# Beginning the first feed-forward with the context's w1 and w3 products, and seven products for every latent pair

## The chip, the cores and the metric

The kernel runs on one core of a Trainium2 chip. Its metric is the device time of one execution in microseconds. Engines are named as in the profile: PE (matrix products), DVE (vector), ACT (activation), POOL (GpSimd), SP (issues most DMAs). One program is one in-order stream for each engine; the streams wait on each other with semaphores.

## The reference, cut to what matters

One layer of a diffusion trunk with 1024 latent tokens and 256 context tokens of width 1024. The change lies in the first of its two feed-forwards, with F = 2816 hidden columns (22 blocks `f` of 128):

```python
def rms_norm(x, w):
    y = x * lax.rsqrt(jnp.mean(x * x, axis=-1, keepdims=True) + EPS)
    return y * w
def modulate(h, shift, scale):
    return h * (1.0 + scale[:, None, :]) + shift[:, None, :]
def swiglu(h, w1, w3, w2):
    return (jax.nn.silu(h @ w1) * (h @ w3)) @ w2

m_l = split(silu(c) @ ada_w + ada_b, 9)          # latents: 9 groups of 1024 modulation columns
m_c = split(silu(c_ctx) @ ada_w + ada_b, 9)      # context
x = x + 0.5 * m_l[2] * swiglu(modulate(rms_norm(x, norm1_w), m_l[0], m_l[1]), ffn1_w1, ffn1_w3, ffn1_w2)
ctx = ctx + 0.5 * m_c[2] * swiglu(modulate(rms_norm(ctx, norm1_w), m_c[0], m_c[1]), ffn1_w1, ffn1_w3, ffn1_w2)
...  # token mixing (retention and gated linear attention), second feed-forward, final norm
```

## The kernel before

All tensors lie transposed in SBUF: features on the 128 partitions, tokens along the free axis. The latents are two groups of 512 tokens (`tg` 0 and 1), the context one of 256 (`tg` 2).

**Products.** A float32 product is made of three products of fp32r parts. `split` makes a high part on ACT (`whi`, `hh`; a copy to fp32r) and a low part, the rest, on DVE or POOL (`wlo`, `hl`; a TENSOR_TENSOR subtraction of the high part from its source). So a block of weights of 128x512 costs one load, one ACT copy and one subtraction before PE can use all of it. `mm3` and `proj` issue hi·hi, hi·lo and lo·hi.

**Classic blocks and pairs.** A block f done the classic way takes w1 and w3, each over 8 slices of the features and 2 token groups: 2 x 8 x 2 x 3 = 96 matmuls of 128x512. A pair of blocks (f, f+1) can instead be done by `chain`, with the seven products of a 2x2 block scheme over sums of weight halves (`seven_w`) and sums of token-group halves (the four T tiles, made once by `t_make`): 7 x 4 x 3 = 84 matmuls for w1 and 84 for w3. One chain's result goes through ACT (silu) or DVE (multiply) into stores to DRAM.

**Opening.** `first1`, with an order for PE, DVE and ACT written by hand, takes f = 0 to 3 the classic way. It begins with the norm of the first latent group and with modulation columns (8, 0, 9, 1, ...) made on PE (`pe_load`, `pe_sums`, `pe_turn`: eight matmuls of a 32-wide condition with a 512 KB block of `ada_w`, then a turn of the row into a column); as soon as the norm's slice 0 is there, blocks 0 to 3 begin for token group 0, slice by slice. Then, in `phase_ffn1`'s loop, the same four blocks follow for token group 1, while `t_make` makes the T tiles on DVE and ACT. Other modulation columns are made on DVE by a custom multiply-and-add reduction over a 128x1024 tile (line 523 in the profile).

**Pairs and the rest.** `hidden(4)` runs the chains of pairs f = 4, 6, ..., 20; then PE does the w2 sums of the latents (`back6`), whose start the prediction uses as a mark. After that `ctx_ffn` does the whole context feed-forward: 44 units of w1 or w3 (24 matmuls of 128x256 each; the weights loaded a second time) with the w2 sums of a pair of blocks between them. In that stretch two low halves of every unit's four are given to POOL (`hl<-s,hh`, line 422). It is followed by products of the second norm.

**Order.** `Recorder` records a stretch of the program, plans an order for all engines from costs of its own (with `LEAD`, a DMA rate of 300 GB/s, a landing time `DLAT`, and DVE and POOL treated as sharing a port), and emits it. Outside recorded stretches a scheduler with priorities orders the instructions.

Of the kernel before, what the change touches and what calls it, by code (L numbers as in the profile page):

```python
# [41 lines left out]
class Root:  # L42
    def __init__(self, shape, dtype, make=None, real=None, pool=None, slot=None, ready=-1e9):
        self.shape, self.dtype, self.make, self.real, self.pool, self.slot = shape, dtype, make, real, pool, slot
        self.log, self.todo, self.end, self.ready = [], 0, ready, ready


class View:
# [25 lines left out]
    def __getitem__(self, key):  # L74
        k = key if isinstance(key, tuple) else (key,)
        dims, off = [], list(self.off)
        for i, (s, n, a) in enumerate(self.dims):
            j = k[i] if i < len(k) else slice(None)
            if isinstance(j, slice):
                b, e, _ = j.indices(s)  # L80
                off[a] += b * n
                dims.append((e - b, n, a))
            else:
                off[a] += j * n
# [81 lines left out]
class Recorder:  # L166
    def __init__(self, trunk):
        t = self.trunk = trunk
        self.nc, self.tc, self.ops, self.group, self.slots, self.kept = t.nc, t.tc, [], None, {}, {}
# [39 lines left out]
    def add(self, eng, call, outs, ins, name, a, k):  # L209
# [4 lines left out]
        if eng == "PE":  # L214
# [5 lines left out]
            else:  # L220
                cost = size / 600 + 0.01 if size > 64 else size * 0.0011
        elif eng == "SP":
# [10 lines left out]
        op.kind = kind  # L233
        op.port = eng == "POOL" or name in SHARED and not any(self.psum(v.root) for v in ins)
# [12 lines left out]
    def link(self):  # L247
        event, touched = None, defaultdict(list)
        for i, op in enumerate(self.ops):
            op.i = i  # L250
            for v, w in [(v, False) for v in op.ins] + [(v, True) for v in op.outs]:
                r, (a, b, c, d) = v.root, v.box
                keep = []
                for e in r.log:
                    (p, q, s, t), o, ow = e
                    hit = p < b and a < q and s < d and c < t
                    hit = hit or self.psum(r) and not (w and ow)
                    if hit and (w or ow) and o is not op:
                        op.pre.add(o)
                    if not (w and a <= p and q <= b and c <= s and t <= d and o is not op):  # L260
                        keep.append(e)
                r.log = keep + [((a, b, c, d), op, w)]
                if r not in op.roots:
# [5 lines left out]
                    if isinstance(r.pool, Pool):  # L269
                        op.pre.add(r.pool.event)  # L270
# [32 lines left out]
    def run(self):  # L303
# [3 lines left out]
        free = {"PE": 0.0, "DVE": LEAD, "ACT": LEAD, "POOL": LEAD, "SP": LEAD}  # L307
        port = {"DVE": LEAD, "POOL": LEAD}
        kind = True
        cand, table, pipe, order = [o for o in self.ops if not o.left], None, LEAD, []  # L310
        while cand:
            best = None
            byeng = defaultdict(list)
            for o in cand:
# [28 lines left out]
            else:  # L343
# [9 lines left out]
                if o.eng == "SP":  # L353
                    pipe = max(pipe, s) + o.bytes / 300e3
                    o.end = max(pipe, s) + DLAT
# [37 lines left out]
class Trunk:  # L393
    def __init__(self, ctx, tc, I, out, outt):
# [9 lines left out]
        self.sds = [self.nc.dram_tensor(f"sd{i}", (2, NP, P, 512), F32, kind="Internal").ap() for i in range(2)]  # L404
        for n, s in (("cgk", (256, CTX)), ("crk", (512, CTX)), ("cgv", (CTX, 512)), ("crv", (CTX, 512)), ("p89d", (P, CTX)), ("s0g", (4, P, P)),
# [24 lines left out]
    def consts(self):  # L430
# [3 lines left out]
        self.ident = self.tile(cp, [P, P], F32, "ident")  # L434
        self.ones = self.tile(cp, [P, P], F32, "ones")
# [6 lines left out]
    def cond_load(self):  # L442
        self.cs = [self.cond_row("c")]
        self.junk = self.tile(self.dp, [P, D], mybir.dt.bfloat16, "junk")

# [5 lines left out]

    def cond_silu(self):
        for o in (0, 512):
            t = self.cs[-1][:, o:o + 512]
            self.nc.scalar.activation(t, t, AF.Silu)

    def pe_cond(self, pool):
# [10 lines left out]
        self.ab1 = self.tile(pool, [P, 2], F32, "ab1")  # L468
        nc.vector.scalar_tensor_tensor(out=self.ab1, in0=self.col("ada_b")[:, 8:10], scalar=1.0, in1=self.col("norm1_w")[:, 0:2],
# [15 lines left out]
    def pe_copy(self, ps, n, pool):  # L485
        s = self.tile(pool, [P, n], F32, f"csum{n}", 256 // n)
        self.nc.scalar.copy(s, ps[:, :n])
        return [s[:, o:o + P] for o in range(0, n, P)]

# [3 lines left out]

    def pe_out(self, j, src, dve=False):
        if dve and j >= 8:
            k, m, ts = j - 8, self.mods, self.nc.vector.tensor_scalar
# [1902 lines left out]
```

## Time and profile before

| | |
|---|---|
| runs | 2087.51, 2082.72, 2086.14 us; median 2086.14 |
| span of the profiled execution | 2087.0 us (no other time is listed for it) |
| first product of the first feed-forward | 15.12 us |
| first chain (f = 4) | 114.37 us |
| `back6` | 460.33 us |
| context stage (`ctx_ffn`) | 642.33 us |
| PE busy, DVE busy over the span | 2071.6 us, 1471.9 us |

The timeline lists each instruction, or a run of equal ones, with its start and its duration; the starts of successive matmuls are closer than their durations, since matmuls are pipelined. The table by windows gives each engine's busy time in a stretch, the granted PE clock (PEclk, 1.00 is full) and the DMA share and rate. A group's row gives duration in ns of one instruction and a count.

### The profile page before, as it was taken

The numbers are of one execution on the slowest core, as the hardware profiler recorded it, in microseconds if no ns is written. First come the engines' busy times: TensorE is split into PE (matmuls) and PEld (weight loads), VectorE is DVE, ScalarE is ACT, GpSimd is POOL, SyncE is SP. The second block draws the span as 40 slices with busy tenths as digits, with TensorE's granted clock in tenths as the row PEclk, the third lists the DMA queues.
The fourth block names the chain that finished last, engine by engine and source line by source line (L and its number), as shares of the span: only waits on it lengthen the run. The fifth ranks groups of instructions, "written<-read, shape, count | busy, mean of one in ns | idle before, by whom it ended". The sixth has DMA issues, their size and how long they took to land.

```text
span 2087.0 us, 34162 instructions
## 1 busy us (share of the span) xinstructions
PE 2071.6 (99%) x12352; PEld 1763.0 (84%) x12352; DVE 1471.9 (71%) x2660; ACT 973.3 (47%) x1818; POOL 199.3 (10%) x195
## 2 busy tenths in 40 slices
PE   9999999999999999999999999999999999999998
PEld 6888888888889999998788988888888888888888
DVE  6889999666776445765577478767776666765586
ACT  5433433435544445566475246444434344344553
POOL 0000000000015665001021001000000000010000
PEclk9999999999999999999999999999999999999999
DMA  9277667449886553674233233242344444477774
GB/s 348 84 241 237 232 217 256 149 165 371 277 289 222 181 183 115 195 219 129 76 108 98 79 91 105 90 162 81 112 156 147 144 163 157 151 235 229 218 237 151
DMA packets 201082, 370.58 MB, mean 178 GB/s; under 512 B 23249, under 2 KB 35921, under 8 KB 200785
## 3 DMA queue, kind: packets, MB, share of 16 engines
q1 hardware_dynamic: 200768, 368.33, 53.7%
q8 instruction: 97, 1.59, 0.3%
q14 instruction: 73, 0.59, 0.1%
q10 hardware_dynamic: 144, 0.07, 0.0%
HBM read 292.68 MB, written 67.24 MB: 172 GB/s over the span
## 4 chain that ended last, share of the span: by engine, by line
PE 77%; DVE 10%; DMA 8%; issue 3%; ACT 1%; SPq 0%; DVEq 0%; POOLq 0%; ACTq 0%
PE psa L147 18%; PE psa L426 10%; PE psa L428 10%; PE psa L427 10%; PE psb L147 9%; PE psb L427 7%; PE psb L428 7%; PE psb L426 7%; DVE junk L523 2%; DVE wlo L422 2%; DMA raw<-in_w 2%; DMA raw<-sd 2%; DVE hl L422 1%; DMA raw<-gd 1%; DMA hl<-sd 1%
## 5 line engine op out<-in xcount | busy, mean ns | idle before, releaser
L421 ACT ACTIVATE whi<-raw 128x512 fp32r<-128x512 f32 x371 | 233.9, 631 | 502.7 <-issue 160.6
L422 DVE TENSOR_TENSOR wlo<-raw,whi 128x512 fp32r<-128x512 f32 x371 | 254.1, 687 | 178.0 <-ACT whi L421 175.6
L426 PE MATMUL psa<-hh,whi 128*128 128x512 f32 x684 | 267.0, 390 | 1.2 <-ACT s L738 0.6
L428 PE MATMUL psa<-hh,wlo 128*128 128x512 f32 x684 | 266.3, 389 | 0.0
L427 PE MATMUL psa<-hl,whi 128*128 128x512 f32 x684 | 266.2, 389 | 0.0
L427 PE MATMUL psb<-hl,whi 128*128 128x512 f32 x568 | 221.6, 390 | 0.5 <-DVE hl L422 0.3
L428 PE MATMUL psb<-hh,wlo 128*128 128x512 f32 x568 | 221.3, 390 | 0.2 <-DVE wlo L422 0.2
L426 PE MATMUL psb<-hh,whi 128*128 128x512 f32 x568 | 221.1, 389 | 0.0
L426 PEld LDWEIGHTS psa<-hh,whi 128*128 128x128 f32 x684 | 128.4, 188 | 28.9 <-ACT s L711 1.7
L147 DVE TENSOR_TENSOR wlo<-raw,whi 128x512 fp32r<-128x512 f32 (+1 forms) x140 | 88.5, 647 | 90.8 <-ACT whi L147 80.1
L147 PE MATMUL psa<-hl,whi 128*128 128x512 f32 x384 | 152.5, 397 | 0.0
L147 PE MATMUL psa<-hh,whi 128*128 128x512 f32 x384 | 152.3, 397 | 0.0
L147 PE MATMUL psa<-hh,wlo 128*128 128x512 f32 x384 | 152.2, 396 | 0.0
L428 PEld LDWEIGHTS psa<-hh,wlo 128*128 128x128 f32 x684 | 128.4, 188 | 26.6
L427 PEld LDWEIGHTS psa<-hl,whi 128*128 128x128 f32 x684 | 128.5, 188 | 26.3
L422 POOL TENSOR_TENSOR hl<-s,hh 128x512 fp32r<-128x512 f32 x88 | 132.4, 1530 | 145.2 <-DVE hl L422 81.1
L147 ACT ACTIVATE whi<-raw 128x512 fp32r<-128x512 f32 (+1 forms) x140 | 82.5, 599 | 119.7 <-PE psa L147 94.1
L427 PEld LDWEIGHTS psb<-hl,whi 128*128 128x128 f32 x568 | 106.6, 188 | 24.7 <-DVE hl L422 2.7
L428 PEld LDWEIGHTS psb<-hh,wlo 128*128 128x128 f32 x568 | 106.6, 188 | 23.1 <-DVE wlo L422 1.2
L426 PEld LDWEIGHTS psb<-hh,whi 128*128 128x128 f32 x568 | 106.6, 188 | 22.2
L428 PE MATMUL psa<-hh,hl 128*128 128x256 f32 x392 | 111.1, 284 | 0.0
L426 PE MATMUL psa<-hh,hh 128*128 128x256 f32 x392 | 111.1, 283 | 0.0
(443 smaller groups left out, 4820.4 us busy)
## 6 DMA issues: line engine op xcount, KB each, us to landing
raw<-in_w SPq DMA_DIRECT2D x242, 256.0 KB, 3.3
s<-in_w SPq DMA_DIRECT2D x198, 256.0 KB, 3.7
gd<-s SPq DMA_DIRECT2D x154, 256.0 KB, 2.8
ada<-in_adaT SPq DMA_DIRECT2D x60, 512.0 KB, 4.6
raw<-gd SPq DMA_DIRECT2D x91, 256.0 KB, 3.5
sd<-s SPq DMA_DIRECT2D x44, 256.0 KB, 2.7
raw<-sd SPq DMA_DIRECT2D x44, 256.0 KB, 3.2
hh<-in_w SPq DMA_DIRECT2D x44, 256.0 KB, 4.0
```

The costliest lines, as they stand in the source:

```text
L147: self.rec.add(self.eng, lambda: f(*map(get, a), **{x: get(v) for x, v in k.items()}), outs, ins, name, a, k)
L421: nc.scalar.activation(hi, src, AF.Copy)
L422: (eng or nc.vector).tensor_tensor(out=lo, in0=src, in1=hi.bitcast(F32), op=ALU.subtract)
L426: mm(ps, wa[0], xa[0], start=start, stop=False, skip_group_check=more)
L427: mm(ps, wa[0], xa[1], start=False, stop=False, skip_group_check=more)
L428: return mm(ps, wa[1], xa[0], start=False, stop=stop, skip_group_check=more)
L523: nc.vector.tensor_tensor_reduce(out=self.junk, in0=t, in1=self.cs[s], scale=1.0, scalar=self.col("ada_b")[:, j:j + 1], op0=ALU.mult, op1= ...
```

## The change

The kernel now opens with the context. `ctx_open` loads the context (1 MB, in a new layout `ctxP`, four loads) ahead of the first column's tile, makes its norm, and makes all 16 columns of modulation groups 0 and 1 on PE (ten before). It then does 14 units (f = 0 to 6) slice by slice into seven PSUM banks, in the order of the table `OPEN`: a pair (i, q) loads half q of unit i, a positive number loads two column tiles, a negative one makes the two columns and the norm of a slice. `ctx_rest` does the remaining 30 units one after the other; of each unit's two 128x512 weight halves one low part is made on DVE and one on POOL. The gated products go to DRAM (`cgd`, 22 stores). Beside it `lat_open`, a generator that is advanced once for each f, issues the latents' loads, squares, norms and `t_make`; in its norms `norm_a` and `norm_b` are one SCALAR_TENSOR_TENSOR each on DVE. All of this is one recorded stretch, planned with a lead of 0, a DMA rate of 345 GB/s, a landing of 2 us, and without the shared port of DVE and POOL (`apart=False`). The first weight halves of `hidden`'s first chain (`seven_w`) are part of it.

Then `hidden(0)` does all eleven pairs by chains. The later `ctx_ffn` does only the w2 sums: it loads w2 and `cgd`. There POOL makes one of four low parts of a pair's w2. Modulation groups 0 and 1 are dropped from the columns made on DVE (72 reductions in place of 84).

```diff
 class Recorder:
-    def __init__(self, trunk):
+    def __init__(self, trunk, lead=None, rate=300e3, land=None, apart=True):
...
-        op.port = eng == "POOL" or name in SHARED and not any(self.psum(v.root) for v in ins)
+        op.port = self.apart and (eng == "POOL" or name in SHARED and not any(self.psum(v.root) for v in ins))
...
+                    if o.eng == "SP" and not self.apart:
+                        t = max(t, pipe - BACKLOG)
...
+    def ctx_open(self, xp, n1):
...
+        for k in range(KD):
+            for i in range(NW):
+                w, h = self.wslice(ws[i], k), self.h[2][k]
+                for j, (u, v) in enumerate(((0, 0), (1, 0), (0, 1))):
+                    nc.tensor.matmul(acc[i], w[u], h[v], start=k + j == 0 and i % 2 == 0, stop=k == KD - 1 and j == 2,
+                                     skip_group_check=True)
+        return acc
+
+    def ctx_g(self, f, p1, p3):
+        t = self.stile()[:, :CTX]
+        self.nc.scalar.activation(t, p1, AF.Silu)
+        self.nc.vector.tensor_tensor(out=t, in0=p3, in1=t, op=ALU.mult)
+        self.nc.sync.dma_start(self.cgd[f], t)
+
+    def ctx_rest(self, xp, n1, lat):
+        acc = self.ctx_open(xp, n1)
+        load = lambda w: [self.load_half(w[:, 512 * q:512 * q + 512], None, self.nc.gpsimd if q else None) for q in range(2)]
+        units = [w[f] for f in range(NW // 2, NF) for w in (self.w1, self.w3)]
+        ws = [load(units.pop(0))]
+        for f in range(NW // 2):
+            self.ctx_g(f, acc[2 * f], acc[2 * f + 1])
+        next(lat)
+        for f in range(NW // 2, NF):
+            ps = []
+            for _ in range(2):
+                if units:
+                    ws.append(load(units.pop(0)))
+                ps.append(self.psA()[:, :CTX])
+                self.proj(ws.pop(0), 2, ps[-1])
+            self.ctx_g(f, *ps)
+            next(lat, None)
+        for _ in lat:
+            pass
...
-            ws = self.first1((xp, xp, None), n1)
-            t_steps = self.t_make(xp, tp)
-            for f in range(4):
-                self.c_silu(f, 1, self.H(ws[2 * f], 1), True)
-                next(t_steps)
-                self.c_mul(f, 1, self.H(ws[2 * f + 1], 1))
-                if f % 2:
-                    next(t_steps)
...
+        rec = Recorder(self, 0.0, 345e3, 2.0, False)
...
+        self.ctx_rest(xp, nn, self.lat_open(xp, nn, swap))
+        ready = self.seven_w(self.w1, 0, True)
+        rec.run()
...
-        self.hidden(4, lambda: mods(MPER), True)
+        self.hidden(0, lambda: mods(MPER), True, ready)
...
-            self.ctx_ffn(units, norms, last)
+            self.ctx_ffn(norms)
...
-PECOL = (8, 0, 9, 1, 2, 3, 4, 5, 6, 7)
+PECOL = tuple(8 * i + k for k in range(8) for i in (1, 0))
-EMODS = ((5, (0,)), (2, (0, 1)), (1, (1,)), (0, (1,)), (4, (0, 1)), (3, (0, 1)), (7, (0,)), (6, (0,)))
+EMODS = ((5, (0,)), (2, (0, 1)), (4, (0, 1)), (3, (0, 1)), (7, (0,)), (6, (0,)))
-WARM = (18, 4)
+WARM = 30
+NW = 14
+BACKLOG = 3
```

In the order of instructions, counted over the whole program, PE loses 48 matmuls of 128x512 and gains 48 of 32x128 (six columns); the number of 128x256 ones by fp32r parts is the same. From the middle of the chains after the context stage on, the order is the same on all engines.

**PE at the start, before.** In these rows line 482 makes the sums of columns 8, 0 and 9, line 491 turns them, line 1198 keeps PE busy, and line 1204 is the first product of the latents.

```order
L482 MATMUL psb_161<-ada_69_197,ccol_185 32x128 x8
L482 MATMUL psa_241<-ada_70_200,ccol_185 32x128 x8
L491 MATMUL psb_159<-cols_80,csum_87_242 128x2
L491 MATMUL psa_162<-cols_80,csum_88_243 128x2
L1198 MATMUL psa_158<-ones_83 128x128 x4
L1204 MATMUL psa_274<-hh_16_114,wh_148 128x512
L1204 MATMUL psa_274<-hh_16_114,wl_149 128x512
L482 MATMUL psb_161<-ada_73_206,ccol_185 32x128 x8
```

**PE at the start, after.** Recorded instructions all carry line 147; `hh_23` is the high part of the context's normed slice 0.

```order
L147 MATMUL psb_175<-ada_17_139,ccol_134 32x128 x8
L147 MATMUL psb_188<-ada_18_148,ccol_134 32x128 x8
L147 MATMUL psb_175<-cols_80,csum_197 128x2
L147 MATMUL psb_188<-cols_80,csum_205 128x2
L147 MATMUL psb_223<-ada_42_161,ccol_134 32x128 x8
L147 MATMUL psa_234<-hh_23_221,whi_202 128x256
L147 MATMUL psa_234<-hh_23_221,wlo_212 128x256
L147 MATMUL psa_234<-hh_23_221,whi_210 128x256
```

The third column's sums stand ahead of the first product now, and the products are of 256 tokens.

**DVE before the first chain, before.** This is the stretch of `t_make` (`t1l`, lines 1119 and 1123) with the first chains' weight parts (`wlo`, line 690) between.

```order
L1119 TENSOR_TENSOR x_131_470<-x_131_470,x_10_93 128x512
L422 TENSOR_TENSOR wlo_1141<-raw_1131,whi_1140 128x512
L690 TENSOR_TENSOR raw_1131<-raw_1137,raw_1131 128x512
L422 TENSOR_TENSOR t1l_184_841<-x_131_470,t1h_183_840 128x512
L1119 TENSOR_TENSOR x_135_515<-x_135_515,x_11_95 128x512
L422 TENSOR_TENSOR wlo_1146<-raw_1137,whi_1145 128x512
L422 TENSOR_TENSOR t1l_186_843<-x_135_515,t1h_185_842 128x512
```

**DVE where the latents' norms begin, after.** `s_1262` is the gate of f = 9 (it needs the sixth of the 30 units from PE); the rows on `x_161` to `x_163` are the first norms, and their group goes on below it for 114 rows in all up to the first chain's w1.

```order
L147 TENSOR_TENSOR wlo_1303<-raw_1164,whi_1290 128x512
L147 TENSOR_TENSOR nacc_1204<-nacc_1204,nsq_1300 128x512
L147 TENSOR_TENSOR nacc_1204<-nacc_1204,nsq_1308 128x512
L147 TENSOR_TENSOR s_1262<-psa_1258,s_1262 128x256
L147 SCALAR_TENSOR_TENSOR x_161_739<-x_161_739,mod_88,nrb_1315 128x512
L147 SCALAR_TENSOR_TENSOR x_162_753<-x_162_753,mod_88,nrb_1315 128x512
L147 SCALAR_TENSOR_TENSOR x_163_767<-x_163_767,mod_88,nrb_1315 128x512
```

The norms and the T tiles now share DVE with the weights' low parts and gates of the context's units.

**POOL, the first large instructions before and after.** Before, the first ones are low parts of the context stage; in after, low parts of the units in `ctx_rest`.

```order
L1665 TENSOR_TENSOR nr_4952<-nr_4952,mhalf_85 128x2
L422 TENSOR_TENSOR hl_1322_5968<-s_5842,hh_1321_5967 128x512
L422 TENSOR_TENSOR hl_1328_5992<-s_5844,hh_1327_5991 128x512
L422 TENSOR_TENSOR hl_1334_6016<-s_5875,hh_1333_6015 128x512
```

```order
L147 TENSOR_TENSOR wlo_843<-raw_727,whi_828 128x512
L147 TENSOR_TENSOR wlo_950<-raw_856,whi_939 128x512
L147 TENSOR_TENSOR wlo_1026<-raw_879,whi_1012 128x512
L147 TENSOR_TENSOR wlo_1086<-raw_899,whi_1070 128x512
```

Of POOL's 88 large subtractions 41 are left: 30 of them stand in the opening, 11 in the context stage.

More of the change, by code (lines that the diff above doesn't have):

```diff
@@ L450, in cond_row @@
         return t
[L452 to L455, printed above, removed]
     def pe_cond(self, pool):
@@ new lines, in ctx_norm, with col_sums @@
+        for t in (acc, sq):
+            for o in (0, CTX):
+                nc.tensor.matmul(pr[:, :CTX], self.ones, t[:, o:o + CTX], start=t is acc and not o, stop=t is sq and o > 0)
+        rb = self.scr(n1, "nacc", 1)[:, :CTX]
+        nc.scalar.activation(rb, pr[:, :CTX], AF.Ln, bias=eps, scale=1.0 / D)
+        nc.scalar.activation(rb, rb, AF.Exp, scale=-0.5)
+        return rb
+    def col_sums(self, pc, o, j, sm, turn, to):
+        self.pe_sums(pc, o, self.cur.pop(j))
+        self.nc.scalar.copy(sm, pc[:, o:o + P])
+        return self.pe_turn(turn, to, sm)
```

549 lines of the change are left out of this document (215 added, 334 removed).

## The prediction, written before the changed kernel was run

> **What bounds the kernel now.** I read the page first: shares of busy time and the slices.
>
> ```profile
> span 2087.0 us, 34162 instructions
> PE 2071.6 (99%) x12352; PEld 1763.0 (84%) x12352; DVE 1471.9 (71%) x2660; ACT 973.3 (47%) x1818; POOL 199.3 (10%) x195
> ...
> DVE  6889999666776445765577478767776666765586
> POOL 0000000000015665001021001000000000010000
> ```
>
> PE is busy for 99% of the span, so on the whole only fewer or cheaper matmuls help. But DVE is at 80 to 90% and more in slices 3 to 7, the opening and the chains of the pairs, and POOL is silent there; it works only in slices 12 to 15, the context stage. Next the table by windows, for four stages (first chain; the other pairs up to `back6`; `back6` with what follows it; context stage) and two samples.
>
> ```profile
> core 0: us, PE busy (x) PEld busy (x) DVE busy (x) ACT busy (x) POOL busy (x), PEclk, DMA share, GB/s
> 114.37:133.42 19.05, 19.05 (x86) 15.78 (x85) 18.64 (x31) 8.31 (x15) 0.00 (x0) 1.00 0.82 271
> 133.42:460.33 326.91, 326.08 (x1430) 267.20 (x1428) 288.51 (x490) 126.28 (x222) 1.64 (x1) 1.00 0.64 212
> 642.33:865.72 223.39, 223.38 (x1741) 217.67 (x1740) 117.30 (x182) 115.63 (x231) 124.73 (x84) 1.00 0.55 179
> 700.00:750.00 50.00, 50.00 (x420) 50.00 (x419) 20.44 (x28) 25.59 (x51) 35.89 (x24) 1.00 0.58 184
> 2.00:30.00 28.00, 25.89 (x197) 17.85 (x196) 16.97 (x34) 17.60 (x33) 0.00 (x0) 1.00 1.02 380
> ```
>
> In the first chain DVE works 18.64 of 19.05 us: PE and DVE bind there together. In the context stage it works only 117.30 of 223.39, with POOL's help. Third, PE's timeline at the stage marks.
>
> ```profile
> start us, us, engine line op out<-in xcount [idle before <-releaser]
> 11.57 0.64 PE L482 MATMUL psb<-ada,ccol 128*32 128x128 f32 x16
> ...
> 15.12 0.50 PE L1204 MATMUL psa<-hh,wh 128*128 128x512 f32 x1 [0.51 <-ACT hh L621]
> ...
> 32.76 0.39 PE L1204 MATMUL psa<-hh,wh 128*128 128x512 f32 x1
> ...
> 37.93 0.39 PE L1204 MATMUL psa<-hh,wh 128*128 128x512 f32 x1
> ...
> 114.37 0.39 PE L426 MATMUL psa<-hh,whi 128*128 128x512 f32 x1
> ...
> 133.41 0.39 PE L426 MATMUL psb<-hh,whi 128*128 128x512 f32 x1
> ...
> 460.33 0.39 PE L426 MATMUL psa<-hh,whi 128*128 128x512 f32 x1
> ```
>
> From these: a chain of 84 matmuls takes 133.41 − 114.37 = 19.04 us, 0.2267 each. The 18 chains up to `back6` take 460.33 − 114.37 = 345.96, or 19.22 each with what they lose. A matmul of 256 tokens takes 50.00 / 420 = 0.119 us (0.1195 when counted over longer stretches). From 32.76 to 37.93 PE does 18 products (4.08) and one column: 1.09 us for a column.
>
> **The balance.** Let T be the start of the first chain after the change. Then 22 chains follow, 422.8 us at 19.22, then the rest, without the context's w1 and w3: 44 units x 24 = 1056 matmuls x 0.1195 = 126.2 us that leave a stage in which PE never waits. So the change in time is T + 422.8 − 460.3 − 126.2 = T − 163.7. All hangs on whether the first chain starts before 163.7 us.
>
> **T by PE alone.** Removed: 8 products x 8 slices x 6 of 512 tokens for f = 0 to 3 (384) against 4 chains (336): 48 x 0.2267 = 10.9 us saved. Added: six columns x 1.09 = 6.5. Start: ahead of the first column stand 1.05 MB of context, where 2.1 MB of latents stood; at the 380 GB/s of the window from 2 to 30 that is 2.8 us earlier, 8.8 for the columns and, with the same 3.55 us from there (15.12 − 11.57), 12.4 for the next work. From there PE has 336 products of 256 tokens (14 units) = 40.2 and 14 columns = 15.3: the opening block ends at 67.9. The 30 other units, 720 x 0.1195 = 86.0, and the small products of two latent norms (some 2 us each, an estimate from the eight of 284 ns and the eight of 239 that one norm takes in the opening, below) end at 157.9. That is T if PE waits for nothing: 157.9 − 163.7 = −5.8, or 2081.2.
>
> ```profile
> L599 PE MATMUL psb<-ndiag,ones 128*128 128x128 f32 x8 | 1.1, 284 | 0.0
> L583 PE MATMUL psb<-ones,nacc 128*128 128x1 f32 x8 | 0.9, 239 | 0.0
> ```
>
> The opening's transfers: 28 weight halves (7.3 MB), 16 column tiles (8.4) and the context (1.0), 16.8 MB, at 380 GB/s 44 us; they land by about 47, and PE is at its last column pair at about 50. That covers it, barely; if PE lost a tenth of the rate, it would wait 4 to 5 us.
>
> **T by DVE.** The order on DVE tells more. Up to the gate of f = 9 (`s_1262`) DVE waits for PE: that row needs six of the 30 units, 67.9 + 17.2, 2.0 for the first norm's products and 0.7 for ACT and the gate itself: 87.8. Only behind it, in DVE's order, stand the latents' norms, the T tiles, ten modulation reductions and the other units' low halves, 114 rows down to the low part of the first chain's w1. Their prices are pitches from DVE's dense timeline and the group of reductions:
>
> ```profile
> 615.87 0.68 DVE L422 TENSOR_TENSOR hl<-hl,hh 128x512 fp32r<-128x512 f32 x1
> 616.47 0.68 DVE L878 TENSOR_TENSOR s<-psa,s 128x512 f32<-128x512 f32 x1
> 617.08 0.74 DVE L884 SCALAR_TENSOR_TENSOR x<-s,mod,x 128x512 f32<-128x512 f32 x1
> 617.74 0.68 DVE L422 TENSOR_TENSOR wlo<-hh,whi 128x512 fp32r<-128x512 f32 x1
> 618.34 0.68 DVE L422 TENSOR_TENSOR hl<-hh,hh 128x512 fp32r<-128x512 f32 x1
> 618.94 4.15 DVE L884 SCALAR_TENSOR_TENSOR x<-s,mod,x 128x512 f32<-128x512 f32 x3
> 623.02 1.77 DVE L422 TENSOR_TENSOR hl<-hl,hh 128x512 fp32r<-128x512 f32 x1
> 624.71 0.74 DVE L884 SCALAR_TENSOR_TENSOR x<-psa,mod,x 128x512 f32<-128x512 f32 x1
> ...
> L523 DVE CUSTOM_DVE_ANT_0 junk<-ada,condc,cols x54: 1266/1276/1286, 24.0 to 362.4; 128x1024 bf16<-128x1024 f32 x54
> ```
>
> 40 SCALAR_TENSOR_TENSOR x 0.66 (617.08 to 617.74) = 26.4; 39 TENSOR_TENSOR x 0.60 = 23.4; 10 gates of 256 elements x 0.34 (their 0.41, below, less the overlap of 0.07 that the larger ones show) = 3.4; 10 reductions x 1.24 (1.276 less some overlap) = 12.4; the last one's end 0.7: 66.3 us. So DVE alone gives 87.8 + 66.3 = 154.1, only 3.8 us less than PE's 157.9. Whatever DVE loses beyond 3.8 us, the first chain starts later, and PE, which runs ahead of its low halves and gates, waits.
>
> **What POOL costs DVE.** 21 of POOL's 30 low halves fall beside these 114 rows. What that costs is seen where POOL's first large instructions begin, at 619.08, in the DVE rows above.
>
> ```profile
> 619.08 6.86 POOL L422 TENSOR_TENSOR hl<-s,hh 128x512 fp32r<-128x512 f32 x4 [81.12 <-DVE hl L422]
> ...
> L422 POOL TENSOR_TENSOR hl<-s,hh x88: 1285/1640/1806, 619.1 to 817.9; 128x512 fp32r<-128x512 f32 x88
> L984 DVE TENSOR_TENSOR s<-psa,s x22: 408/410/425, 651.0 to 829.5; 128x256 f32<-128x256 f32 x22
> ```
>
> From 618.94 to 624.71 DVE does three SCALAR_TENSOR_TENSOR and one TENSOR_TENSOR, 2.58 us by pitch, in 5.77: 3.19 lost to about three POOL instructions, 1.06 each. The 22 gates that read one PSUM operand stay at 408 to 425 ns while POOL runs; those don't pay. Of the 66 us some 50 (the first two terms, two SBUF operands) are like those that pay, so I take 0.75 x 1.06 = 0.80 for each: 21 x 0.80 = 16.8. Ends: 0 (if POOL always falls beside reductions and gates; a gain is excluded, since POOL's 21 halves are not among DVE's rows any more) and 22.3 (1.06 each). So T = 154.1 + 16.8 = 170.9, +7.2 against 163.7, 2094.2 by the profiled span. The median of the runs is 0.9 below that span: 2093.3.
>
> [...]
>
> **Small parts.** SP: each of the 22 stores of a gate waits for DVE, and the weights of later units are queued behind it; the loads behind `s_1262`'s store serve units five or six further on, 15 us of PE work, while landing takes 3 to 4, so I price it at nothing; without that cover each store would cost PE up to 3 us. ACT has some 60 us of copies, squares and norms in 90 us of `ctx_rest`: hidden. The context stage after: per pair PE has 48 x 0.1195 = 5.7 us, DVE 3 low parts and a split (2.4), the loads 1.3 MB (3.4 at 380 GB/s): hidden; uncovered, it would cost under 1 us per pair. The 12 reductions that go (15 us of DVE) lie in the last chains, where DVE has air: nothing, at best 1 us.
>
> **The rivals.** (1) *PE stays the bound*: POOL falls beside gates, reductions and DVE's waits. T = 157.9, 2081.2, as a median 2080. For it: PE's 99%; against it: DVE's 154.1 leaves 3.8 us, so it decides at 0.18 us per POOL instruction, a sixth of what the row shows. (2) *Half the contention*, 0.45 us each: T = 154.1 + 9.5 = 163.6, no change, 2086. For it: POOL's instructions take 1.64 at the median against 1.285 alone, so part of the conflict is paid by POOL. (3) *PE waits and its clock falls*. After two waits of 0.21 and 1.63 us the trace has this:
>
> ```profile
> 1024.60 0.33 PE L147 MATMUL psb<-zq,zk 128*32 128x32 f32 x16 [1.63 <-issue]
> ...
> 1025.00:1027.00 2.00, 2.00 (x23) 1.57 (x19) 1.96 (x5) 0.34 (x2) 0.00 (x0) 0.59 0.03 8
> 1027.00:1029.00 2.00, 2.00 (x49) 1.28 (x49) 0.51 (x3) 0.39 (x3) 0.00 (x0) 0.56 0.00 0
> ```
>
> Granted clock 0.59 and 0.56 for 4 us: 1.7 us of work lost. If PE waits 13 us in `ctx_rest` in pieces of 1 to 3, five such episodes cost 8.5: 2102. The waits will rather be short, one per unit, and PE's work has slack behind DVE then; so less likely. [...] (4) *The opening doesn't feed PE*: transfers at nine tenths of the rate, +5 on rival 1's way, hidden on DVE's only in part: 2086 to 2100, within the others.
>
> **How the numbers follow.** DVE bound with contention, 2087 to 2099 (0.3 to 1.06 us each), 0.46; rival 1 0.26; rival 2 0.18; rival 3 0.10. 0.2%, about what a measurement here tells from no change, is 4.2 us: faster is under 2082, slower over 2090.3. Faster is rival 1: 0.26. Same: rival 2 and 0.04 of the first case, 0.22. Slower: 0.42 + 0.10 = 0.52. The time is that of the likeliest, 2093. The range takes in rival 1 with 3 us of uncertainty on PE's sum (2077.5) and ends at rival 3's 2102.5; some 1 in 10 lies on either side.
>
> **What the profile after would show.** First product at 12.4; the last of the 14 units at 67.9 (if it is later than 72, the transfers bound it). First chain at 171; `back6` 423 us later, at 594. In 90 to 170 us DVE busy over 95% and PE at 85 to 90%, its waits ended by DVE's low halves or POOL's; DVE's `wlo` rows there at about 1 us in place of 0.685, POOL's at 1.6. Wrong would be: PE without waits up to 158 (rival 1); DVE's rows at 0.69 beside POOL; a granted clock under 0.9 between 90 and 170 (rival 3); or a loss behind `back6`, where I expect none.

## The result, and the profile after

The changed kernel takes 2119.3 us (median of four runs, 2119.03 to 2120.25) against 2085.4 for the kernel before: a ratio of 1.0167, interval 1.0152 to 1.0181. It is slower, as forecast, but by 34 us where 7 had been predicted. The page of the changed kernel, its head and three of its rows over the 40 slices:

```profile
span 2117.2 us, 34420 instructions
...
PE 2077.4 (98%) x12438; PEld 1776.4 (84%) x12438; DVE 1516.4 (72%) x2710; ACT 986.3 (47%) x1820; POOL 133.7 (6%) x148
...
DVE  5799999766666577774678467868866676665676
ACT  4644334343344545565665345534433434344553
POOL 0341000000000002011011102000000000010000
```

The span is 30.2 us longer, and PE's busy time only 5.8 us: the rest is PE's waiting. (A run's time lies some 2 us above its span, 2119.03 and 2117.2 here. So the profiled execution before, with a span of 2087.0, was one of about 2089, over 3 us above the median of its kernel; the prediction compared the two without this step and put the median 0.9 below the span. For this reason the account below adds up to 30 us and not to 34.) POOL now works in slices 2 to 4 of the opening. PE's timeline at the marks (start, duration, instruction):

```profile
15.28 0.47 PE L147 MATMUL psa<-hh,whi 128*128 128x256 f32 x1 [0.77 <-ACT hh L147]
...
187.49 0.40 PE L439 MATMUL psa<-hh,whi 128*128 128x512 f32 x1
...
211.32 0.39 PE L439 MATMUL psb<-hh,whi 128*128 128x512 f32 x1
...
611.88 0.39 PE L439 MATMUL psa<-hh,whi 128*128 128x512 f32 x1
```

These are the first product, the first chain, the second chain and `back6`. Together with the ends of the stages they give this account. `prod(4)` is the one product of the latents' w2 sums that is left for after the context stage; 126.2 us of work moved from the context stage to the front:

| stretch | before, us | after, us | change |
|---|---|---|---|
| to `back6` | 460.3 + 126.2 | 611.9 | +25.4 |
| `back6` and what follows it | 182.0 | 179.5 | -2.5 |
| context stage with prod(4) | 223.4 - 126.2 | 108.2 | +11.0 |
| the rest, to PE's last matmul | 1214.4 | 1210.9 | -3.5 |

So two stretches are to be explained. Of the last row 1.7 us is the half clock near 1025 us that the prediction shows in the trace before; the clock of the trace after is full throughout this stretch up to PE's last matmuls. The rest of that row and the second row were not followed up. For the first stretch, the table by windows of the changed kernel:

```profile
core 0: us, PE busy (x) PEld busy (x) DVE busy (x) ACT busy (x) POOL busy (x), PEclk, DMA share, GB/s
10.00:30.00 20.00, 18.73 (x207) 15.38 (x207) 9.87 (x22) 9.51 (x21) 0.00 (x0) 0.83 1.04 396
30.00:68.00 38.00, 38.00 (x406) 36.34 (x405) 27.10 (x51) 22.52 (x44) 3.24 (x2) 1.00 0.83 297
68.00:95.00 27.00, 25.21 (x207) 24.61 (x207) 16.63 (x28) 16.23 (x32) 11.19 (x8) 1.00 0.81 259
95.00:187.50 92.50, 77.34 (x572) 75.95 (x571) 86.07 (x115) 44.91 (x81) 37.60 (x22) 0.89 0.64 209
```

From 95 us to the first chain DVE is busy for 93%, and PE waits 15.2 us and runs at a granted clock of 0.89, which costs another 8.5. PE's list of waits from 12 to 200 us says for whom (us in total, times, longest; two entries of under 1 us are left out):

```profile
PE psa L147 <- DVE wlo L147: 11.2, 4, 5.1
PE psb L147 <- DVE ndiag L147: 5.7, 5, 3.2
PE psa L439 <- ACT s L703: 2.9, 1, 2.9
```

These are DVE's low halves, the small scalings (`ndiag`) of the latents' norms, and an ACT copy (`s`) inside the first chain. And DVE's groups from the gate of f = 9, done at 93.7, to the first chain show why it is late (busy us and mean ns stand after the count):

```profile
L147 DVE TENSOR_TENSOR wlo<-raw,whi 128x512 fp32r<-128x512 f32 x22 | 19.1, 882 | 0.9 <-ACT whi L147 0.9
L510 DVE CUSTOM_DVE_ANT_0 junk<-ada,condc,cols 128x1024 bf16<-128x1024 f32 x10 | 14.6, 1462 | 0.1
L147 DVE SCALAR_TENSOR_TENSOR x<-x,mod,nrb 128x512 f32<-128x512 f32 x16 | 14.5, 938 | 1.5 <-ACT nrb L147 1.5
L147 DVE SCALAR_TENSOR_TENSOR hl<-x,mod,hh 128x512 fp32r<-128x512 f32 x12 | 11.7, 997 | 0.0
L147 DVE TENSOR_TENSOR s<-psa,s 128x256 f32<-128x256 f32 x11 | 4.5, 414 | 3.0 <-PE psa L147 3.0
L147 DVE TENSOR_SCALAR ndiag<-ident,nr 128x128 f32<-128x128 f32 x4 | 3.0, 780 | 0.9 <-POOL nr L147 0.9
```

`wlo` takes 882 ns on average, the norm's instructions 938 and 997, where 684 and 745 are their times alone (shown with the second experiment); the gates, with one operand in PSUM, take 414, where those of the kernel before took 410 at the median. Row by row, 21 instructions are lengthened, 20.3 us together, and POOL does 21 subtractions in this stretch. Each of the 21 began while POOL was in a subtraction, and its extra time is what was left of that subtraction, less 0.13 or 0.19 us. One pair of rows, from the timelines of POOL and DVE:

```profile
103.78 2.46 POOL L147 TENSOR_TENSOR wlo<-raw,whi 128x512 fp32r<-128x512 f32 x1 [2.42 <-ACT whi L147]
105.02 1.76 DVE L147 SCALAR_TENSOR_TENSOR hl<-x,mod,hh 128x512 fp32r<-128x512 f32 x1
```

The subtraction (2.46 us here, where the shortest in the kernel before took 1.29, so POOL loses time too) ends at 106.24, 1.22 us after the DVE row began, and this row takes 1.02 us longer than the 0.74 of its kind.

### The profile page after: what moved, and what is told of

Same layout as the page of the kernel before. It is cut to its first block, busy times and chain, and to the rows that moved or that the text cites. A ratio compares the mean times of both kernels' runs of the same rounds, so it can differ in the third digit from the quotient of the medians.

```text
span 2117.2 us, 34420 instructions
## 1 busy us (share of the span) xinstructions
PE 2077.4 (98%) x12438; PEld 1776.4 (84%) x12438; DVE 1516.4 (72%) x2710; ACT 986.3 (47%) x1820; POOL 133.7 (6%) x148
## 4 chain that ended last, share of the span: by engine, by line
PE 90%; DVE 5%; DMA 3%; ACT 1%; issue 1%; POOL 0%; SPq 0%; POOLq 0%; DVEq 0%; ACTq 0%
PE psa L147 21%; PE psa L439 10%; PE psa L440 10%; PE psa L441 10%; PE psb L147 10%; PE psb L440 9%; PE psb L441 9%; PE psb L439 9%; DMA raw<-in_w 2%; DVE x L147 1%; DVE hl L147 1%; DVE wlo L147 1%; PE psa L1962 0%; DVE wlo L435 0%; DVE nt L147 0%
## 5 line engine op out<-in xcount | busy, mean ns | idle before, releaser
L439 PE MATMUL psa<-hh,whi 128*128 128x512 f32 x692 | 269.4, 390 | 2.1 <-ACT hh L434 1.5
L440 PE MATMUL psa<-hl,whi 128*128 128x512 f32 x692 | 269.4, 389 | 0.4 <-DVE hl L435 0.4
L441 PE MATMUL psa<-hh,wlo 128*128 128x512 f32 x692 | 269.4, 389 | 0.0
L147 PE MATMUL psa<-hh,wlo 128*128 128x512 f32 (+1 forms) x648 | 230.9, 357 | 11.2 <-DVE wlo L147 11.2
L147 PE MATMUL psa<-hh,whi 128*128 128x512 f32 (+1 forms) x648 | 230.7, 357 | 0.8 <-ACT hh L147 0.8
L147 PE MATMUL psa<-hl,whi 128*128 128x512 f32 (+1 forms) x648 | 230.2, 356 | 0.0
L147 ACT ACTIVATE whi<-raw 128x512 fp32r<-128x512 f32 (+1 forms) x209 | 125.1, 608 | 151.6 <-PE psa L147 103.5
L439 PEld LDWEIGHTS psa<-hh,whi 128*128 128x128 f32 x692 | 129.8, 188 | 29.6 <-ACT hh L434 1.7
L440 PEld LDWEIGHTS psa<-hl,whi 128*128 128x128 f32 x692 | 129.9, 188 | 27.6 <-DVE hl L435 0.9
L441 PEld LDWEIGHTS psa<-hh,wlo 128*128 128x128 f32 x692 | 129.9, 188 | 27.0
L147 PEld LDWEIGHTS psa<-hh,wlo 128*128 128x128 f32 x648 | 126.7, 196 | 26.1 <-DVE wlo L147 11.9
L147 PEld LDWEIGHTS psa<-hh,whi 128*128 128x128 f32 x648 | 126.5, 195 | 16.8 <-ACT hh L147 1.0
L147 PEld LDWEIGHTS psa<-hl,whi 128*128 128x128 f32 x648 | 126.5, 195 | 14.1 <-issue 0.2
```

The lines of the kernel that those rows point to most:

```text
L147: self.rec.add(self.eng, lambda: f(*map(get, a), **{x: get(v) for x, v in k.items()}), outs, ins, name, a, k)
L439: mm(ps, wa[0], xa[0], start=start, stop=False, skip_group_check=more)
L440: mm(ps, wa[0], xa[1], start=False, stop=False, skip_group_check=more)
L441: return mm(ps, wa[1], xa[0], start=False, stop=stop, skip_group_check=more)
```

## Experiments on the opening

Theory A: DVE's in-order stream sets the first chain, and POOL's instructions hold it up. Rivals: loads, or PE's own stream.

**All low halves on DVE.**

```diff
-        load = lambda w: [self.load_half(w[...], None, self.nc.gpsimd if q else None) for q in range(2)]
+        load = lambda w: [self.load_half(w[...], None, None) for q in range(2)]
```

> All low halves of the 30 units of ctx_rest are made on DVE, none on POOL. In the trace of the changed kernel 21 DVE instructions between the gate of f = 9 (93.4 us) and the first chain (187.5) lasted 0.66 to 1.14 us longer than their kind, 20.3 us together, each beside one POOL instruction. Theory A (DVE's in-order stream sets the start of the first chain, and POOL's instructions hold it up): DVE gains 20.3 and takes on 21 x 0.60 = 12.6, first chain at about 180, time about 2111 to 2113, and no DVE TENSOR_TENSOR of 512 over 0.75 us there. Rival B (loads, which wait on SP for buffers, or PE's own stream set it): first chain within 2 us of 187.5, time 2118 to 2121. If the long DVE instructions are only waits by another name, DVE just gets 12.6 us more: first chain at 200, 2131.

2103.9 us, ratio 1.0087 (1.0072 to 1.0102), first chain at 173.96: 13.5 us earlier, though DVE does 30 instructions more. The same window of this kernel:

```profile
95.00:187.50 92.50, 83.66 (x614) 79.87 (x613) 89.01 (x153) 51.28 (x94) 1.40 (x1) 0.96 0.68 221
```

No DVE row is lengthened any more (`wlo` takes 684 ns on average, the norm's instructions 743 and 746). The gain is larger than theory A's 7.7 (20.3 less 12.6 for 21 more low halves): the gate of f = 9 also came 1.4 us earlier, and DVE's waits behind it fell from 6.3 to 3.3 us; PE's clock is 0.96 in place of 0.89. The rivals fall.

**POOL's instructions stay, but read nothing.** The low part of one half of each unit's weights is left out; POOL writes zeros in its place.

```diff
+        if eng and self.blank:
+            eng.memset(lo.bitcast(F32), 0.0)
+        else:
             (eng or nc.vector).tensor_tensor(out=lo, in0=src, in1=hi.bitcast(F32), op=ALU.subtract)
```

> Opening and context stage as changed, but the low part that POOL makes of half of every unit's weights is left out: POOL writes zeros there (a memset), in the same places, and reads nothing. So DVE has the same work as in the changed kernel and POOL's instructions stay in number. Theory A with its mechanism (a DVE instruction with two SBUF operands waits while a POOL instruction reads SBUF): no DVE instruction of 512 elements over 0.8 us in 94 to 187 us, first chain at 187.5 - 20.3 = 167, to 172 if PE's waits set it, time 2098 to 2104. Rival (the long DVE instructions come from POOL's writes or its mere presence, or cost nothing): some stay long, first chain after 178, 2110 to 2121.

2105.0 us, ratio 1.0089 (1.0074 to 1.0105), first chain at 171.52. DVE's groups from 87 us to there, the same kinds as above:

```profile
L147 DVE TENSOR_TENSOR wlo<-raw,whi 128x512 fp32r<-128x512 f32 x23 | 15.4, 684 | 0.9 <-ACT whi L147 0.7
L513 DVE CUSTOM_DVE_ANT_0 junk<-ada,condc,cols 128x1024 bf16<-128x1024 f32 x10 | 12.8, 1276 | 0.0
L147 DVE SCALAR_TENSOR_TENSOR x<-x,mod,nrb 128x512 f32<-128x512 f32 x16 | 11.3, 745 | 0.2 <-ACT nrb L147 0.2
L147 DVE SCALAR_TENSOR_TENSOR hl<-x,mod,hh 128x512 fp32r<-128x512 f32 x12 | 8.7, 745 | 0.5 <-ACT hh L147 0.5
L147 DVE TENSOR_TENSOR s<-psa,s 128x256 f32<-128x256 f32 x11 | 4.6, 418 | 0.1
L147 DVE TENSOR_SCALAR ndiag<-ident,nr 128x128 f32<-128x128 f32 x7 | 2.3, 414 | 0.0
```

Every kind with two operands in SBUF is back at its time alone. From the gate of f = 9 to the first chain it is 74.2 us in place of 94.1, though the gate itself came 3.9 us later, behind a wait of DVE for ACT. `ndiag` is not back: three of these scalings took 0.52 to 0.64 us, each beside a memset, where 0.28 is the time without POOL (283 ns on average in the experiment before).

POOL's memsets are shorter (528 ns) than its subtractions, so this run changes two things, reading and length. The rows separate them: six DVE instructions with two operands in SBUF began with 0.27 to 0.43 us of a memset left, more than the 0.13 to 0.19 that go free beside a subtraction, and none took 0.01 us longer than alone. So both experiments show that POOL's subtractions cost DVE its time, and this one that for two operands it is their reading. (The trace is that of the fastest of this kernel's four runs, 2100.8 us.)

**The reductions behind the opening.**

```diff
-                nc.scalar.activation(t[:, o:o + 512], t[:, o:o + 512], AF.Silu)
+                v = nc.scalar.activation(t[:, o:o + 512], t[:, o:o + 512], AF.Silu)
+                tc.add_manual_dep(v.ins, rec.last["DVE"], SCHED, reason="order")
```

> The reductions of modulation columns on DVE wait until the recorded opening's last DVE instruction, so the ten that stand ahead of the first chain's w1 move behind it; POOL's halves stay. Theory A: DVE's stream ahead of the first chain loses 10 x 1.24 = 12.4 us and some of its contention, first chain at about 174 to 176; the reductions find room in later chains, time about 2106 to 2109. Rival B (loads or PE): first chain within 2 us of 187.5, time 2118 to 2121. Rival D (the reductions only move the loss): first chain at 175, but the chains behind it lose the 12 us, 2118 to 2121.

2111.8 us, ratio 1.0124 (1.0109 to 1.0139). The first chain came at 182.24, only 5.3 us earlier where 12 were expected: the gate of f = 9 came 1.7 us later, and DVE's waits behind it were 11.5 us in place of 6.3. So the reductions had partly filled time in which DVE waits anyway. PE's wait inside the first chain is gone, and `back6` came at 602.20, 9.7 earlier. Not the loads, then; theory A with too large a price.

**Both.**

> Both: all low halves on DVE, and the ten reductions behind the opening. Theory A: 187.5 - 7.7 - 12.4 = 167 for the first chain, close to what PE needs by itself (157.9 as forecast, and 6 us for the late start and the half clock at the opening, 164), time about 2098 to 2101. Rival B: first chain within 3 us of 187.5, time 2117 to 2121.

2101.2 us, ratio 1.0075 (1.0058 to 1.0092), first chain at 169.03, `back6` at 589.47. Against the balance of the prediction (`back6` at 586.5 for no change) the front is now 3 us late and not 25.

**Idle matmuls for the clock.**

```diff
+                for _ in range(8):
+                    nc.tensor.matmul(p[:, 2 * P:3 * P], self.ones, self.ones, start=True, stop=True)
```

> Eight idle matmuls of 128x128 stand behind the turn of the first two columns, where the kernel before had eight of its own. In the changed kernel the granted clock from 10 to 30 us was 0.83 over 18.7 busy us, 3.2 us of work; the kernel before had 1.00 there. Theory A (the anchor of DVE's stream, the gate of f = 9, waits for PE, so what PE loses here moves the first chain): granted clock 1.00 from 10 to 30, first chain 2 to 3 us earlier (185), time 2116 to 2117. Rival: the clock falls for another reason, or PE's loss is absorbed before the gate: clock 0.8 still, or first chain at 187.5, 2118 to 2121.

2122.7 us, ratio 1.0168 (1.0152 to 1.0183), no gain. The clock was 1.00 from 10 to 30 us and the first chain at 185.59, but `back6` at 611.27, only 0.6 earlier: in the first chain (up to 215 us) the clock was 0.88, where the changed kernel had 0.94. The clock is not a reliable sign either: kernels with the same opening as the changed one showed 1.00, 0.91, 0.74 and 0.83 in these 20 us, and their first chains lay between 183.9 and 187.5, so a difference of 3 us at that mark means nothing by itself.

**The latents' norms earlier in DVE's order.** The generator of the latents' work is advanced three times before the 30 units, so that the norms stand behind the gate of f = 7 in place of f = 9.

```diff
-        next(lat)
+        for _ in range(3):
+            next(lat)
         for f in range(NW // 2, NF):
```

> The changed kernel with that one edit (latents' work advanced three times before the units), POOL's halves and the reductions where the change put them. Theory A: the gate that stood ahead is now that of f = 7, some 10 us earlier; DVE's sum behind it stays, so the first chain moves from 187.5 to 178 to 182, and the time to 2110 to 2114. Rival (POOL's contention just fills the time): 2117 to 2121.

2118.4 us, ratio 1.0153 (1.0136 to 1.0169), first chain at 184.0 where 178 to 182 was expected. The norms did begin 13.2 us earlier (80.50 in place of 93.72), but this gained 3.5 us. The run doesn't settle the question by itself: DVE then stood 5.3 us, up to 182.26, before a reduction whose tile had not landed. With the mends of the next section's last run, in which the reductions stand behind the opening:

> As the fastest version so far (low halves on DVE, reductions behind, late high part, latent norm of the context stage a pair later; 1.0053 of before), and the generator of the latents' work is advanced three times in place of once before the 30 units, so that in DVE's order the latents' norms begin behind the gate of f = 7 in place of f = 9. Theory A's anchor (norms and T tiles stand behind a gate that waits for PE, while DVE had idle time before it): the first chain comes 4 to 8 us earlier, 163 to 167, time 2089 to 2093 where before is 2086. Rival (PE alone sets the first chain by now, with 158 and the losses of the start): first chain within 2 us of 170.8, 2095 to 2098.

2096.3 us, ratio 1.0047 (1.003 to 1.0063), first chain at 170.31 against 170.84 in that last run, though the norms began at 76.92 in place of 90.38. So the gate as an anchor is not what remains. ACT's waits from 60 to 175 us in the second of these kernels:

```profile
ACT whi L147 <- DMA raw<-in_w: 19.8, 14, 4.6
ACT whi L147 <- PE psa L147: 12.2, 16, 1.8
```

Without POOL and the reductions ACT waits for weights to land, and the loads wait in SP's queue for buffers that DVE's low halves free (46 us of SP's waits). I read this as a round trip between the engines; PE is still 12 us behind its own sum of 157.9. This is a reading of rows and not shown: more buffers, which would test it, were not tried.

## Experiments on the context stage

PE's first product of this stage, ACT's instruction that holds it up, and the two windows around (the clock is the column after POOL):

```profile
797.68 0.58 PE L439 MATMUL psb<-ghi,hh 128*128 128x256 f32 x1 [6.12 <-DVE s L871]
...
795.68 0.63 ACT L434 ACTIVATE whi<-raw 128x512 fp32r<-128x512 f32 x1 [9.65 <-DMA raw<-in_w]
...
791.40:799.40 8.00, 1.88 (x9) 1.72 (x9) 3.06 (x6) 3.23 (x6) 0.94 (x1) 0.64 0.55 187
799.40:807.40 8.00, 7.87 (x50) 7.67 (x49) 7.70 (x13) 5.44 (x10) 0.35 (x1) 0.72 0.68 213
```

PE waits for four DVE instructions (`s`, line 871) that free the PSUM banks; ahead of them on DVE stands a low half of prod(4)'s fourth weight, whose high half ACT can't make before the weight lands; its load stood in SP behind loads of w2 that waited for buffers. PE waits 8.2 us in the whole stage, and loses about 3 more at a low clock: the 11 us of the account. What is the cause, one misplaced instruction, or the missing cover (the w1 and w3 products, which gave these loads, splits, drains and the norm time to finish)?

**prod(4)'s weights without priority**

> Opening as changed. The weights of the product after the context stage (prod(4)) lose their priority of 150, so that one low half (waiting for a weight that landed at 795.6 us) no longer stands on DVE ahead of the four instructions that free the PSUM banks for the context's w2 sums. PE waited 6.1 us for these, and its granted clock was 0.63 and 0.80 in the two windows to 810. If this one instruction is the cause of the 11 us lost in the context stage: time 2108 to 2112, and no wait of PE over 1 us at the stage's start. If the stage is late for its own loads (w2 behind waits on SP): PE waits there still, 2116 to 2121.

2120.3 us, ratio 1.0165 (1.015 to 1.018), no gain. DVE's instruction moved, and PE waited 5.7 us for the norm's sum (`nacc`) in its place.

**The norm's parts later**, for the counts (0, 0, 1, 1, 1, 1, 1, 1, 2, 2) of its ten parts behind the ten pairs:

```diff
-            norms.pop(0)()
+            for _ in range((0, 0, 1, 1, 1, 1, 1, 1, 2, 2)[p]):
+                norms.pop(0)()
```

> In the context stage the parts of the second latent norm come behind the third and later pairs' w2 sums in place of the first and later. Theory E (the w1 and w3 units that stood here before, 4 of them or 12 us ahead of the norm's first matmul, covered the way from back6's last product over the sums to that matmul; without them PE reaches it first): the wait on nacc that showed when the weight was moved does not come back, but here the weight still stands ahead of the PSUM drain, so PE still waits some 6 us at the stage's start, and time is 2117 to 2121. Under the rival that the norm's place alone causes the wait: 2108 to 2112.

2122.2 us, ratio 1.0168 (1.0151 to 1.0185): PE waited 4.5 us for the drain (the four instructions `s`) and 2.4 for low parts of the context's gated products (`glo`). Both edits together:

> Both edits of the context stage: prod(4)'s weights without priority, and the norm's parts later. Theory E (two waits in parallel, one behind the other: moving either alone only lets the other show): no wait of PE over 1.5 us at the stage's start, granted clock 1.00 there, 9 to 11 us gained, time 2108 to 2111. Rival (the stage is late for its loads of w2): a third wait takes the place, 2116 to 2121.

2125.0 us, ratio 1.0172 (1.0155 to 1.0189), no gain where 9 to 11 us were expected: PE waited 6.6 us for `glo`. ACT still stood before the late weight; only DVE's half had moved.

**The fourth weight's high half behind the fifth pair's, on ACT**

```diff
+            if i == 4 and p == 3 and self.late:
+                self.tc.add_manual_dep(self.act.ins, self.late, SCHED, reason="order")
```

> Opening as changed. In the traces of both edits of the context stage ACT still stood in front of one high part of prod(4)'s fourth weight until it landed at 796 us, with the second pair's high parts (hh) and the squares of the norm queued behind it; its load is held in SP behind loads of the third pair that wait for buffers. Here that one high part is put behind the fifth pair's high parts in ACT's order; nothing else moves. Theory F (this one ACT instruction holds DVE's low parts, the PSUM drain and the norm): no wait of PE over 2 us at the stage's start, 8 to 11 us gained, time 2108 to 2112. Rival (the stage has no cover any more: whatever comes last, w2's loads or the norm, shows): a wait of 4 to 6 us stays, 2116 to 2121.

2115.8 us, ratio 1.0144 (1.0129 to 1.0159): about 5 us better than the changed kernel where 8 to 11 were expected. The stage has 2.3 of them (105.9 us in place of 108.2); most of the rest is in the front, which has the same order. A wait remains, so the single instruction was not the cause, only the last of several:

```profile
PE psa L570 <- DVE nacc L561: 3.7, 1, 3.7
PE psa L439 <- ACT hh L434: 1.5, 1, 1.5
```

**Idle matmuls in place of the cover**

```diff
+            if not p:
+                w, t, ps = self.cw[0][0], self.cw[0][1], self.psA()
+                for i in range(48):
+                    self.nc.tensor.matmul(ps[:, :CTX], w[i % 4][...], t[0][0], start=i == 0, stop=i == 47)
```

> As the changed kernel, with 48 idle matmuls of 256 tokens (5.74 us) between back6 and the first w2 sums of the context stage; their sums are used for nothing. They need the first pair's parts as the sums do, and no bank of those that are drained. Theory G (the 11 us of the context stage are the chain of loads, splits, drain and norm that the w1 and w3 units used to cover): the idle matmuls run in PE's wait, the clock stays up, and the time changes by -3 to +2 us, 2117 to 2122. Rival (PE's wait is set by something that moves along with PE's work, as its own products' loads would): +5 to +6, 2124 to 2126.

By the profile the lost cover is the cause: PE has 5.74 us more work, and the stage takes 108.5 us in place of 108.2. The wait for the drain is gone, and one of 2.3 us for `nacc` shows. But the trace is that of the fastest run. The times, 2124.3 us, ratio 1.0178 (1.0159 to 1.0196), are some 2 us above those of the changed kernel by the ratio, with overlapping intervals and runs from 2120.7 to 2128.9; their median lies in the range expected of the rival. So the cover is the likelier account, and not shown by the times.

**Mends together.** All edits of the opening with prod(4)'s priority and the norm's parts later; then both edits of the opening with the late high half; then that with the norm's parts at counts (0, 1, 1, 1, 1, 1, 1, 1, 1, 2):

> All edits together: low halves on DVE, reductions behind the opening, eight idle matmuls, prod(4) without priority, the norm's parts later. If the losses add: 2101 (both edits of the opening) less 9 to 11 in the context stage and 0 to 3 for the clock = 2087 to 2092, about the kernel before. If they hide behind each other (a wait moved is a wait elsewhere): 2095 to 2101.

> Both edits of the opening (low halves on DVE, reductions behind) and the late high part. If theory F holds and the losses add: 1.0075 x before less 8 to 11 us, 2090 to 2094 where before is 2086. Rival: 2099 to 2102.

> As the run before, and the norm's parts one pair later. If a wait for the norm's sum (nacc) remains with the late high part: 1 to 3 us faster than that run. If none remains: the same within 1.5 us.

2104.4 us, ratio 1.0078 (1.0063 to 1.0093); 2099.8, 1.0069 (1.0054 to 1.0084); 2096.8, 1.0053 (1.0036 to 1.007). The first lies above both ranges that were expected, the second in its rival's. The losses do not add as hoped: the context stage kept 105.5 to 111 us in all of them against 97.2 before. None beats the kernel before.

## Why the prediction was wrong, point by point

- **Which steps failed.** Two terms carry nearly all of the miss. The first chain, forecast for 170.9, came at 187.5: 16.6 us in T by DVE, namely 5.9 in the gate that it starts from, 6.3 in DVE's waits, which it put at nothing, and 3.5 in POOL's price. And the context stage, which "Small parts" put at nothing, lost 11.0.
- **The direction and its mechanism** held: the chains take over as in the balance (`back6` 424.4 us behind the first chain, 422.8 forecast), DVE sets the first chain, and POOL's low halves are the largest single cause. With them off DVE's way the front gains 17 us (`back6` 611.9 to 594.9).
- **What POOL costs DVE** was sized at 16.8 us, with 22.3 as the upper end; it measured 20.3. What was wrong is the factor of 0.75, by which a quarter of the subtractions would have cost nothing: against 21 subtractions stand 21 lengthened rows. The reductions took 1462 ns on average in place of 1276, and `ndiag` 780 where 283 is its time without POOL. Its own row's 1.06 us for each was close to the 0.97 measured. The 1.29 of POOL's shortest subtraction before, 27 us for 21, would have been too much: each of the 21 rows paid what was left of a subtraction, less 0.13 or 0.19 us.
- **T by DVE** was 87.8 + 66.3. The gate was done at 93.7 and not at 87.8. The 14 units ended at 70.6 in place of 67.9, about as late as the first product (15.28 in place of 12.4); the clock of 0.83 from 10 to 30 us cost some 3 us more (0.17 of 18.73), so other terms of PE's sum were too large by as much. The bytes were right: the first column's tile, forecast for 8.8, landed at 8.7. But in PE's order idle matmuls on `ones` and the context norm's sums stand ahead of the columns:

```profile
4.61 5.36 PE L1962 MATMUL psa<-ones 128*128 128x128 f32 x44
9.81 1.03 PE L147 MATMUL psb<-nacc,ones 128*128 128x256 f32 x4
10.67 1.03 PE L147 MATMUL psb<-nsq,ones 128*128 128x256 f32 x4
11.63 1.08 PE L147 MATMUL psb<-ada,ccol 128*32 128x128 f32 x32
```

  From the 14 units to the gate it took 23.1 us in place of 19.9; PE waited 1.8 of them. Behind the gate come 6.3 us of DVE's waits for PE, ACT and POOL, which a sum of DVE's rows leaves out: two engines that wait for each other in turn take longer than the busier one. With contention these make 15.7 of the 16.6 us by which the first chain missed 170.9. This is an account along DVE's order. That an earlier gate would bring the first chain as much earlier is not shown: 13.2 us of earlier norms brought 3.5.
- **Small parts, the context stage**: priced at nothing, it cost 11 us. I compared DVE's and the loads' work per pair with PE's (2.4 and 3.4 against 5.7 us) and found them covered. That holds in the steady pairs. But the start of the stage is a chain of drain, norm, loads and splits, and its end is the hand-over to prod(4); some 12 us of w1 and w3 products (four units) before each pair's sums had covered these. PE's waits of 8.2 us and its low clock make up the 11; that the lost cover is behind them is the likelier account and not fully shown. DVE is busy for 83 of 108 us there, where it was 117 of 223.
- **Rivals.** PE as the bound, and half the contention, fell. So did an opening that doesn't feed PE: it was busy for 38.00 of 38.00 us from 30 to 68. The clock (rival 3) came in beside the likeliest case and not in place of it: 8.5 us from 95 to 187.5. Each case was priced alone; the upper end of contention and rival 3 together gave 2107, which the range did not allow for.
- **Loads behind stores in SP**, priced at nothing, cost nothing that PE's list of waits shows: no wait of PE there ends with a load. With the mends SP waits mostly for buffers of low halves (46 us from 60 to 175) and less for the gates' stores (16).

## What to carry to other kernels

Work that is moved out of a stage takes its cover along: list what is hidden there (drains, a norm's chain, first loads, the hand-over to the next stage), not only the busy time per step. When two engines are within a few per cent of binding, price the waits between them on top of the busier one's sum. And before work is given to POOL, ask what DVE does at that moment: in the context stage before, at 52% of DVE, 88 subtractions on POOL were hidden (PE was busy for 223.38 of 223.39 us); in the opening, at 93%, each of 21 cost it nearly a microsecond.

## What the runs showed of the hardware

In the changed kernel, from the gate of f = 9 to the first chain, 21 DVE instructions that began beside a POOL subtraction of 128x512 were lengthened by 0.66 to 1.14 us, which is the rest of the subtraction less 0.13 to 0.19 us in each of the 21 rows. Among them are two scalings of one SBUF tile (`ndiag`, 1.28 and 1.30 us in place of 0.27) and two of the custom reductions (2.32 and 2.10 us in place of 1.28). Gates with an operand in PSUM were not lengthened: the four that began beside a subtraction took 0.41 us (414 ns is the mean of all, 418 in the run with POOL's memsets). Nor were five rows with two SBUF operands (0.68 us each) that began with 1.8 us or more left of a subtraction that itself took 2.1 to 2.7 us. Beside POOL's memsets nothing with two SBUF operands was lengthened (684 and 745 ns on average), but scalings were (up to 0.64 us in place of 0.28). 20.3 us over 21 instructions is 0.97 us each, less than the 1.29 of the shortest POOL subtraction before, since DVE's instruction began when part of the subtraction was over.

The clock was granted at 0.64 and 0.72 around a wait of 6.1 us, and at 0.74 to 1.00 from 10 to 30 us with the same instructions in different runs; at the 0.83 of the changed kernel PE's longest wait there was 0.77 us. What sets the clock in that stretch is not shown by these runs.
